# A second planner that alternates backward and forward rounds, and six banks of exponentials, in a two-layer streaming encoder step

## The chip, the cores and the metric

The kernel runs on one core of one Trainium2 chip. The metric is the device time of one execution in microseconds; lower is better. The kernel before took 3009.69 us as the median of three runs (3009.36 to 3010.79).

## The reference

The function is one inference step of a two-layer hybrid encoder for 1024 prompt tokens and 8 x 16 sample tokens (1152 rows, width 1024). All inputs and outputs are float32. Each layer does the following to `x`:

```
h = RMSNorm(x) @ w_in                      # split among three parallel groups
A: gMLP:  gelu(u) * (tril(W_s) @ RMSNorm(gelu(v)) + b_s)      4 groups x 64, chunks of 128
B: conv:  swish(LayerNorm(depthwise_conv31(a * sigmoid(gate))))              width 256
C: latent attention: 8 heads, q and k RMS-normed and rotated, keys and values from a
   128-wide latent, mask in blocks of 64 frames; the sample group also reads a past of 128
x += concat(A, B, C) @ w_out
x += softmax(qm @ mem_k) @ mem_v @ w_mo    # 4 heads x 128 into 256 memory tokens
x += relu(RMSNorm(x) @ w_ff1)^2 @ w_ff2    # hidden 4096
```

It returns `x` for both groups and the new caches (latent, rotary keys, conv state, memory keys and values, gMLP rows).

## The kernel before

A product that needs float32 accuracy is done as three TensorE matmuls: each operand is split into a high part, rounded to the type `float32r`, and a low part, and `mm3` adds high x high, high x low and low x high in one PSUM bank. Smaller products (softmax weights times values, transposes, statistics) are plain float32 matmuls. All matmuls are issued by the helper `mm` (L707) and all transposes by `tr` (L730). The other lines that the profile names are helpers, too: ScalarE activations `act` (L589) and copies (L606), VectorE two-operand instructions `vtt` (L610), `stt` (L679), reductions `red` (L683), scalar instructions `vts` (L671), splits (L750), GpSimd two-operand instructions `ptt` (L614) and memsets (L695), and DMAs on SyncE's queue (L699).

Each layer runs in stages: the mixer's input products; the attention stage, in which the gMLP, the convolution, the latent attention of four pairs of heads, the sample group's attention and the early parts of the out-projection overlap; the rest of the out-projection; memory cross-attention; and the feed-forward part, in which the up-projection uses a scheme with seven products instead of eight.

Some parts of the attention stage matter here. `attention` makes query, key and value rows per tile of 128 tokens ("tok"): matmuls, then sums of squares on ScalarE, an addition on VectorE, a power on GpSimd (`small_rstd`), scaling on ScalarE, rotation on VectorE. `heads` then transposes those tiles on TensorE. `maxima` finds the row maxima of the scores. `units` computes scores of 256 queries against 256 keys in one PSUM bank and their exponentials into a buffer of 512 words; `values` multiplies these with the values. `PTS` bounds how many such buffers of exponentials exist between `units` and `values` (L1978). `mix` is the gMLP's spatial product; its operand passes through a power on GpSimd (`pow_rstd`), too. `conv` runs 31 taps per half as VectorE instructions of 128x1024 (`stt`) for the prompt, and `taps` runs 31 for the sample group, each a ScalarE scaling and a GpSimd addition of 128x128. The result of the convolution goes to the out-projection's last part (`mixer_out`, since `REST` holds parts 2, 3, 6 and 7).

The order of all this is planned twice, while the program is built. The first planner (`plan`) runs the parts above as coroutines with priorities against a table of costs: it places every instruction at a time, and gives out the buffers of two arenas in SBUF (21000 and 36048 words per partition) and the eight PSUM banks. The list `trace` holds its instructions with their times. The second planner (`fix_order`) finds what each instruction must wait for, from the buffers and banks that it reads and writes, so that a reuse of a buffer is kept as the first planner had it. It then lets `in_order` simulate the engines again, SyncE's DMAs as an engine of their own: at each step the engine that is free first takes, of its instructions that are ready, the one with the lowest key. The result is an order for each engine, and it is fixed by dependences. The simulation has TensorE's clock (`array`), instructions that use part of the array (`narrow`), and VectorE and GpSimd that hold each other up (`holds`). The key before is

```
key = [t - URGE * r for (t, _), r in zip(self.trace, rest)]      # URGE = 0.05
```

where `t` is the first planner's time and `rest` the longest chain of costs and delays from the instruction to the end.

Of the kernel before, what the change touches and what calls it, by code (L numbers as in the profile page):

```python
# [41 lines left out]
QK = 10240  # L42
PTS = 5
FK = 3072
# [25 lines left out]
TICK = 10240.0 / 3  # L70
WARM = 3060
URGE = 0.05

# [199 lines left out]
class Enc:  # L273
# [39 lines left out]
    def array(self, t, cost, cols):  # L313


        c0 = cols / cost
        if t < self.tick * TICK:
            self.tick, self.cols_out = 0, 0.0
        while True:
            i = int(t // TICK)  # L320
            if i > self.tick:
                self.warm = i == self.tick + 1 and self.cols_out >= WARM
                self.tick, self.cols_out = i, 0.0
            f = 1.0 if self.warm else 2.0
            d = min(cost * f, (i + 1) * TICK - t)
            cost -= d / f
            self.cols_out += c0 * d / f
            if cost < 1e-6:
                return t + d
            t = (i + 1) * TICK + 1e-6  # L330
# [23 lines left out]
    def fix_order(self):  # L354


        n = len(self.trace)
# [31 lines left out]
        prev = {}  # L389
        for i in self.in_order(preds):  # L390
            ins = self.trace[i][1]
            if ins.engine in prev:
                self._after(ins, prev[ins.engine])
            prev[ins.engine] = ins
# [11 lines left out]

    def in_order(self, preds):
        n = len(self.trace)
        succ, left, ready = [[] for _ in range(n)], [len(p) for p in preds], [0.0] * n
        for i, p in enumerate(preds):  # L410
            for j in p:
                succ[j].append(i)
        engs = {r[0] for r in self.real}
        rest = [0.0] * n
        for i in reversed(range(n)):
            e = self.real[i][0]
            rest[i] += self.real[i][1]
            for j in preds[i]:
                rest[j] = max(rest[j], rest[i] + (0.0 if e == "PE" == self.real[j][0] else BEHIND[self.real[j][0]]))
        key = [t - URGE * r for (t, _), r in zip(self.trace, rest)]  # L420
        soon, now, free = {e: [] for e in engs}, {e: [] for e in engs}, {e: 0.0 for e in engs}
# [4 lines left out]
        while len(out) < n:  # L426
# [27 lines left out]
            else:  # L454
# [6 lines left out]
                free[e] = end  # L461
            out.append(i)
            for j in succ[i]:
                left[j] -= 1
                if e != "PE" or self.real[j][0] != "PE":
                    ready[j] = max(ready[j], end + BEHIND[e])
                if not left[j]:
                    heapq.heappush(soon[self.real[j][0]], (ready[j], j))
        return out

# [2388 lines left out]
```

## Time and profile before

| | us |
|---|---|
| median of three runs | 3009.69 |
| the profiled execution's own time | 3009.8 |
| its span, first to last instruction | 3008.0 |
| TensorE busy | 2920.9 (97%) |
| VectorE busy | 2118.2 (70%) |
| ScalarE busy | 1417.4 (47%) |
| GpSimd busy | 357.1 (12%) |
| mean granted TensorE clock | 0.979 |

In the profile PE is TensorE, PEld its weight loads, DVE VectorE, ACT ScalarE, POOL GpSimd and SP SyncE, whose queue issues the DMAs. A matmul's end is modelled, and TensorE's work is pipelined, so "busy" is not "at its peak". A granted clock of 1.00 is 2.4 GHz and 0.5 is 1.2 GHz. A wait is put down to the instruction that released it; "issue" means that the profile shows no releaser. The attention stages lie at about 150 to 526 us (layer 0) and 1654 to 2030 us (layer 1), the feed-forward stages at about 677 to 1504 and 2181 to 2970 us.

### The profile page before, as it was taken

The page shows a single profiled execution, that of the slowest core. Times are in us where ns is not written, and L with a number is a line of the kernel's source. Part 1 is how long each engine was busy: PE and PEld are TensorE (multiplying, and loading weights), DVE is VectorE, ACT ScalarE, POOL GpSimd, SP SyncE. Part 2 cuts the span into 40 slices and gives each one's busy share as a digit, 9 for nine tenths or more (in the row PEclk, how much of TensorE's full clock was granted, in tenths as well). Part 3 has the DMA queues.
Part 4 walks back from the last instruction along what each step waited for, and adds up shares of the span by engine and source line. Part 5 has one row for each costly group of instructions (what it writes and reads, how often), then busy time and mean ns, then how long its engine had stood idle before and what let it go on. Part 6 is the DMA issues. An engine that isn't in the chain of part 4 may idle for free.

```text
span 3008.0 us, 52427 instructions
## 1 busy us (share of the span) xinstructions
PE 2920.9 (97%) x19708; PEld 2807.8 (93%) x19708; DVE 2118.2 (70%) x4568; ACT 1417.4 (47%) x3762; POOL 357.1 (12%) x427
## 2 busy tenths in 40 slices
PE   8989999999999999999999789999999999999999
PEld 8988988979999999999999688989799999999999
DVE  8986767668655577677898867676687555777775
ACT  7566775466544452111364666664665444521110
POOL 0743220000000000000044422120100000000000
PEclk9989998999999999999999889999999999999999
DMA  6302215433232254222333010453333323532221
GB/s 208 113 30 79 66 45 166 153 120 120 101 125 95 106 185 126 90 90 76 111 99 96 26 36 28 136 182 124 123 113 125 110 91 119 181 121 90 90 73 64
DMA packets 156110, 318.14 MB, mean 106 GB/s; under 512 B 22864, under 2 KB 79824, under 8 KB 155600
## 3 DMA queue, kind: packets, MB, share of 16 engines
q1 hardware_dynamic: 155856, 314.79, 31.4%
q8 instruction: 155, 2.54, 0.3%
q14 instruction: 99, 0.81, 0.1%
HBM read 225.94 MB, written 88.80 MB: 105 GB/s over the span
## 4 chain that ended last, share of the span: by engine, by line
PE 87%; DVE 6%; ACT 4%; POOL 1%; issue 1%; DMA 0%; SPq 0%; DVEq 0%; POOLq 0%; ACTq 0%
PE bank L707 84%; PE bank L730 3%; ACT arena_f L589 3%; DVE arena_f L679 1%; POOL arena_f L614 1%; DVE arena_f L610 1%; DVE arena_r L610 1%; DVE arena_f L683 1%; DVE arena_r L679 1%; ACT arena_r L589 1%; ACT L582 0%; DVE arena_r L750 0%; ACT arena_r L606 0%; DVE arena_f L671 0%; DVE bank L691 0%
## 5 line engine op out<-in xcount | busy, mean ns | idle before, releaser
L707 PE MATMUL bank<-arena_r 128*128 128x384 f32 (+7 forms) x16464 | 2671.5, 321 | 38.8 <-DVE arena_r L750 9.3
L707 PEld LDWEIGHTS bank<-arena_r 128*128 128x128 f32 (+2 forms) x16464 | 2539.8, 190 | 103.8 <-ACT arena_f L589 21.2
L610 DVE TENSOR_TENSOR arena_f<-arena_f,bank 128x384 f32<-128x384 f32 (+1 forms) x1286 | 667.3, 529 | 409.9 <-PE bank L707 404.5
L606 ACT CAST arena_r<-arena_f 128x512 fp32r<-128x512 f32 (+5 forms) x547 | 387.8, 729 | 866.9 <-PE bank L707 799.2
L610 DVE TENSOR_TENSOR arena_r<-arena_f,arena_r 128x512 fp32r<-128x512 f32 (+7 forms) x608 | 496.3, 827 | 148.9 <-PE bank L707 124.3
L589 ACT ACTIVATE arena_f<-arena_f 128x384 f32<-128x384 f32 (+5 forms) x628 | 374.8, 620 | 230.0 <-DVE arena_f L610 171.4
L614 POOL TENSOR_TENSOR arena_f<-arena_f 128x128 f32<-128x128 f32 (+6 forms) x298 | 327.3, 1106 | 837.0 <-DVE arena_f L610 284.6
L589 ACT ACTIVATE arena_f<-bank,arena_f 128x64 f32<-128x64 f32 (+7 forms) x774 | 272.6, 424 | 202.1 <-PE bank L707 68.7
L610 DVE TENSOR_TENSOR arena_f<-arena_f 128x384 f32<-128x384 f32 (+11 forms) x832 | 299.0, 371 | 71.5 <-ACT arena_f L589 62.8
L589 ACT ACTIVATE arena_f<-bank 128x64 f32<-128x64 f32 (+6 forms) x682 | 207.7, 349 | 82.6 <-PE bank L707 44.0
L707 PE MATMUL bank<-arena_f 128*128 128x65 f32 (+7 forms) x2344 | 228.4, 290 | 11.1 <-issue 7.9
L679 DVE SCALAR_TENSOR_TENSOR arena_f<-arena_f 128x1024 f32<-128x1024 f32 (+3 forms) x236 | 221.2, 949 | 3.9 <-POOL arena_f L614 1.6
L707 PEld LDWEIGHTS bank<-arena_f 128*128 128x128 f32 (+2 forms) x2344 | 188.1, 158 | 30.7 <-issue 14.0
L730 PE MATMUL bank<-arena_f 128*128 128x128 f32 (+2 forms) x900 | 162.3, 287 | 33.4 <-ACT arena_f L589 23.8
L730 PEld LDWEIGHTS bank<-arena_f 128*128 128x128 f32 (+2 forms) x900 | 111.7, 142 | 61.4 <-ACT arena_f L589 31.4
L695 POOL MEMSET arena_f<- 128x8 f32 (+3 forms) x125 | 30.6, 251 | 973.5 <-DVE arena_r L610 760.7
L606 ACT COPY arena_f<-bank 128x288 f32<-128x288 f32 (+4 forms) x272 | 104.7, 387 | 76.0 <-PE bank L707 62.4
L683 DVE TENSOR_REDUCE arena_f<-bank 128x1 f32<-128x512 f32 (+4 forms) x224 | 119.4, 555 | 10.2 <-PE bank L707 9.5
L589 ACT ACTIVATION_READ_ACCUMULATOR arena_f<-bank 128x1 f32 x396 | 94.1, 275 | 0.0
L610 DVE TENSOR_TENSOR arena_r<-bank,arena_r 128x256 fp32r<-128x256 f32 (+3 forms) x114 | 57.8, 511 | 34.6 <-ACT arena_r L606 33.6
L679 DVE SCALAR_TENSOR_TENSOR arena_r<-bank,arena_f,arena_r 100x512 fp32r<-100x512 f32 (+3 forms) x92 | 65.9, 725 | 17.9 <-ACT arena_r L589 17.2
L589 ACT ACTIVATE arena_r<-bank,arena_f 100x512 fp32r<-100x512 f32 (+3 forms) x92 | 61.7, 690 | 28.6 <-PE bank L730 28.3
(24 smaller groups left out, 538.6 us busy)
## 6 DMA issues: line engine op xcount, KB each, us to landing
arena_f<-w SPq DMA_DIRECT2D x140, 512.0 KB, 3.6
hscr<-arena_f SPq DMA_DIRECT2D x64, 576.0 KB, 3.2
arena_f<-hscr SPq DMA_DIRECT2D x96, 384.0 KB, 3.6
xscr<-arena_f SPq DMA_DIRECT2D x96, 192.0 KB, 1.9
arena_f<-xscr SPq DMA_DIRECT2D x48, 384.0 KB, 4.1
arena_f<-xscr SPq DMA_DIRECT2D x72, 192.0 KB, 2.5
xscr<-arena_f SPq DMA_DIRECT2D x36, 384.0 KB, 2.3
arena_f<-mkc SPq DMA_DIRECT2D x32, 256.0 KB, 3.1
```

The source lines that it names most:

```text
L589: i = self.nc.scalar.activation(out, in_, func, **kw)
L606: self.nc.scalar.copy(out, in_)
L610: self.nc.vector.tensor_tensor(out=out, in0=a, in1=b, op=op)
L614: self.nc.gpsimd.tensor_tensor(out=out, in0=a, in1=b, op=op)
L679: self.nc.vector.scalar_tensor_tensor(out, a, s, b, op0=o0, op1=o1)
L683: self.nc.vector.tensor_reduce(out, in_, axis=AX.X, op=op, **kw)
L695: self.nc.gpsimd.memset(ap, val)
L707: self.nc.tensor.matmul(out, a, b, start=start, stop=stop, **kw)
L730: self.nc.tensor.transpose(out, in_, self.ident)
```

## The change

`PTS` goes from 5 to 6. In the second planner `URGE` and the sum `rest` are gone. `best_order` calls `in_order` seven times. The first time the key is the first planner's time. `in_order` now also returns when each instruction ends. `latest` then simulates the engines backward from the end: an instruction is ready when all that depend on it are placed, and of the ready ones of an engine that with the latest end in the forward round is taken; its key for the next forward round is its start in that backward schedule, counted back from the end (a negative number, the lowest for what must start first). The backward round uses the recorded costs and delays, without the clock, the narrow matmuls' columns and the engines' mutual hold. Of the seven orders the one whose last instruction ends first is kept. `array`'s state is set back at the start of each round instead of by a comparison of times.

```diff
-PTS = 5
+PTS = 6
...
-URGE = 0.05
+ROUNDS = 7
...
         c0 = cols / cost
-        if t < self.tick * TICK:
-            self.tick, self.cols_out = 0, 0.0
         while True:
...
         prev = {}
-        for i in self.in_order(preds):
+        for i in self.best_order(preds):
             ins = self.trace[i][1]
...
-    def in_order(self, preds):
+    def best_order(self, preds):
+        key = [t for t, _ in self.trace]
+        best = None
+        for _ in range(ROUNDS):
+            out, ends = self.in_order(preds, key)
+            if best is None or max(ends) < best[0]:
+                best = max(ends), out
+            key = self.latest(preds, ends)
+        return best[1]
+
+    def latest(self, preds, ends):
         n = len(self.trace)
+        left, ready = [0] * n, [0.0] * n
+        for p in preds:
+            for j in p:
+                left[j] += 1
+        engs = {r[0] for r in self.real}
+        soon, now, free = {e: [] for e in engs}, {e: [] for e in engs}, {e: 0.0 for e in engs}
+        for i in range(n):
+            if not left[i]:
+                heapq.heappush(soon[self.real[i][0]], (0.0, i))
+        start, todo = [0.0] * n, n
+        while todo:
+            t, e = min((free[e] if now[e] else max(free[e], soon[e][0][0]), e) for e in engs if now[e] or soon[e])
+            while soon[e] and soon[e][0][0] <= t:
+                i = heapq.heappop(soon[e])[1]
+                heapq.heappush(now[e], (-ends[i], i))
+            _, i = heapq.heappop(now[e])
+            _, cost, _, tile = self.real[i]
+            free[e] = t + (30.0 if tile else cost)
+            start[i] = -free[e]
+            todo -= 1
+            for j in preds[i]:
+                left[j] -= 1
+                ej = self.real[j][0]
+                ready[j] = max(ready[j], free[e] + (0.0 if e == "PE" == ej else BEHIND[ej]))
+                if not left[j]:
+                    heapq.heappush(soon[ej], (ready[j], j))
+        return start
+
+    def in_order(self, preds, key):
+        n = len(self.trace)
+        self.tick, self.cols_out, self.warm = 0, 0.0, False
+        ends = [0.0] * n
         succ, left, ready = [[] for _ in range(n)], [len(p) for p in preds], [0.0] * n
...
         engs = {r[0] for r in self.real}
-        rest = [0.0] * n
-        for i in reversed(range(n)):
-            e = self.real[i][0]
-            rest[i] += self.real[i][1]
-            for j in preds[i]:
-                rest[j] = max(rest[j], rest[i] + (0.0 if e == "PE" == self.real[j][0] else BEHIND[self.real[j][0]]))
-        key = [t - URGE * r for (t, _), r in zip(self.trace, rest)]
...
             out.append(i)
+            ends[i] = end
...
-        return out
+        return out, ends
```

## Rows read from the trace of the kernel before

**Rows 1.** Page, parts 1 and 2: TensorE's busy time; granted clock in 40 slices.
```profile
PE 2920.9 (97%) x19708; PEld 2807.8 (93%) x19708; DVE 2118.2 (70%) x4568; ACT 1417.4 (47%) x3762; POOL 357.1 (12%) x427
...
PEclk9989998999999999999999889999999999999999
```

**Rows 2.** Busy time by stretch: stretch, its length, busy us (instructions), clock, DMA share, GB/s.
```profile
150.40:526.40 376.00, 348.96 (x2742) 319.65 (x2741) 274.03 (x844) 250.90 (x1050) 107.23 (x144) 0.92 0.24 77
1654.40:2030.40 376.00, 334.15 (x2603) 305.03 (x2602) 264.40 (x835) 242.99 (x1012) 102.32 (x131) 0.92 0.24 82
676.80:1504.00 827.20, 826.59 (x5440) 823.97 (x5439) 565.90 (x1020) 311.87 (x510) 0.26 (x2) 1.00 0.33 111
2180.80:2932.80 752.00, 752.00 (x5015) 750.41 (x5014) 506.27 (x898) 279.17 (x446) 0.00 (x0) 1.00 0.33 111
```

**Rows 3.** Waits of TensorE: who waited for whom, us in total, times, longest.
```profile
PE bank L730 <- ACT arena_f L589: 23.8, 15, 11.0
PE bank L707 <- DVE arena_r L750: 9.3, 1, 9.3
...
PE bank L707 <- issue: 7.9, 1, 7.9
```

**Rows 4.** Busy time in stretches at clock 0.5: layer 0's sum; layer 1's first and sum.
```profile
sum 58.03, PE 49.08 PEld 43.39 DVE 52.78 ACT 39.49 POOL 19.69; mean PE 8.18 PEld 7.23 DVE 8.80 ACT 6.58 POOL 3.28
...
1670.03:1690.51 20.48, 14.66 (x101) 13.18 (x103) 17.16 (x44) 12.91 (x68) 10.80 (x14) 0.77 0.00 1
...
sum 61.43, PE 53.20 PEld 47.11 DVE 47.77 ACT 35.86 POOL 22.77; mean PE 7.60 PEld 6.73 DVE 6.83 ACT 5.12 POOL 3.25
```

**Rows 5.** Timeline, 1645 to 1685 us: start, length, engine, instructions, idle time before and releaser.
```profile
1659.98 11.59 DVE L679 SCALAR_TENSOR_TENSOR arena_f<-arena_f 128x1024 f32<-128x1024 f32 x9
...
1660.14 16.41 POOL L614 TENSOR_TENSOR arena_f<-arena_f 128x1 f32<-128x1 f32 x13 [0.27 <-DVE arena_f L671]
...
1663.27 0.70 PE L707 MATMUL bank<-arena_f 128*64 128x128 f32 x4 [7.90 <-issue]
1666.31 0.22 ACT L589 ACTIVATE arena_f<-bank 128x64 f32<-128x64 f32 x1 [5.69 <-POOL arena_f L614]
...
1671.48 0.42 DVE L610 TENSOR_TENSOR arena_f<-arena_f 128x6 f32<-128x6 f32 x1
...
1674.32 1.10 ACT L589 ACTIVATE arena_f<-bank,arena_f 128x64 f32<-128x64 f32 x5 [2.62 <-POOL arena_f L614]
...
1674.94 0.64 PE L730 MATMUL bank<-arena_f 128*100 128x128 f32 x2 [10.97 <-ACT arena_f L589]
```

**Rows 6.** Groups by form on VectorE, 1640 to 1680 us: busy, mean ns, idle before.
```profile
L679 DVE SCALAR_TENSOR_TENSOR arena_f<-arena_f 128x1024 f32<-128x1024 f32 x22 | 30.3, 1378 | 0.4
```

**Rows 7.** Groups by form on GpSimd, 1640 to 1680 us.
```profile
L614 POOL TENSOR_TENSOR arena_f<-arena_f 128x128 f32<-128x128 f32 x28 | 29.1, 1040 | 2.0
```

**Rows 8.** Busy time by stretch, around the crowded windows and where VectorE has time.
```profile
400.00:425.00 25.00, 25.00 (x240) 24.36 (x240) 9.93 (x37) 15.63 (x52) 5.76 (x14) 1.00 0.11 38
425.00:450.00 25.00, 19.09 (x162) 16.65 (x160) 15.05 (x65) 25.00 (x142) 10.46 (x11) 0.86 0.11 39
450.00:475.00 25.00, 18.74 (x68) 13.85 (x67) 24.43 (x68) 12.64 (x29) 3.59 (x5) 0.59 0.27 81
...
1740.00:1800.00 60.00, 54.67 (x448) 49.54 (x448) 33.38 (x115) 41.04 (x188) 17.59 (x26) 0.88 0.13 39
```

**Rows 9.** Groups by form on TensorE, whole span: products of exponentials and values.
```profile
L707 PE MATMUL bank<-arena_f 128*128 128x65 f32 x1152 | 146.5, 275 | 1.0 <-ACT arena_f L589 0.8
```

**Rows 10.** Chain of waits, 1640 to 1740 us: start, length, what.
```profile
1645.12 0.54 POOL arena_f L614
1645.73 1.34 POOL arena_f L614
...
1660.06 1.20 DVE arena_f L679
...
1667.40 1.38 DVE arena_f L679
```

## The prediction, made before the changed kernel was run

> **What bounds the kernel now.** I read the page's busy shares first, then the slices of the span, then who TensorE waited for, then busy time by stage, and last the timeline and the chain of waits around the longest stall.
>
> The page [rows 1] is to show one thing: TensorE is busy 2920.9 of 3008.0 us, and its granted clock is full almost everywhere, with dips in slices 3 to 7 of 40 (150 to 526 us) and again in slices 23 to 27 (1654 to 2030 us). Those are the attention stages of layer 0 and layer 1. The table by stage [rows 2] says it in numbers. The feed-forward stage of layer 0 has 826.59 us of TensorE in 827.20, that of layer 1 has 752.00 in 752.00, both at clock 1.00: no order of the same instructions can take anything from them. The attention stages, windows of 376.00 us each, have 348.96 and 334.15 us busy: 27.0 and 41.9 us idle, 68.9 together, out of 87.1 in the span. The remaining 18 us lie mostly at the start (the first matmul waits 9.3 us for its first weights [rows 3]) and at the end behind the last matmul.
>
> The second loss is the clock. Thirteen stretches in the two stages were granted 0.5, that is 1.2 instead of 2.4 GHz; they last 58.03 and 61.43 us, with TensorE busy for 49.08 and 53.20 of these [rows 4]. Work that is done at half clock would take half the time at the full one, so at most (49.08 + 53.20) / 2 = 51.1 us lie there. What order can reach is thus 68.9 + 51.1 = 120.0 us at the very most.
>
> The waits [rows 3] name ScalarE ahead of a transpose first: 23.8 us in 15 waits, 11.0 of it in one. The other large single one is 7.9 us with no releaser shown. Both lie in one place of layer 1 [rows 5]: between 1655.4 and 1674.9 TensorE did 0.70 us of work, 18.9 us of idle. The reader is to see the queues of the other two engines there. VectorE ran nine instructions in one go for 11.59 us, eight of them taps of the depthwise convolution (128x1024); GpSimd ran 13 instructions for 16.41 us; ScalarE stood 5.69 us and later 2.62 us behind GpSimd; and the 128x6 addition that the query/key norm needs came out of VectorE only at 1671.48, behind the taps. From 1640 to 1680 the taps are 22 instructions and 30.3 us of VectorE's 40 [rows 6], and GpSimd's 128x128 additions (the convolution of the sample group) 28 and 29.1 us [rows 7]. The result of the convolution is used only in the last part of the out-projection, at about 2030 us. So work with hundreds of microseconds of slack stood ahead of a chain that TensorE was waiting for. That is what the key of the second planner does: it is the first planner's time less 0.05 of the remaining path (line 420), and an instruction that has fallen behind its planned time has an early key, however little hangs on it.
>
> **The change part by part.** It adds and removes no arithmetic. The rounds only re-order each engine's queue, SP's with its DMAs among them, which is planned as an engine too.
>
> *The 18.9 us stall.* With the latest start in the key, taps and sample additions sink behind the short chains. What is left of the wait is the chain's own steps on GpSimd, which nothing shortens: one power for the gating norm and two for the token norms, at 16.41 / 13 = 1.26 us each [rows 5], 3.8 us. Saved: 18.9 - 3.8 = 15.1 us; bounds 0 (the buffers' reuse holds the taps where they are) and 18.9.
>
> *The half clock behind it.* The stretch 1670.03 to 1690.51 was at 0.5, with 14.66 us of TensorE in it [rows 4]. It began after the long idle time; without that I take the full clock: 14.66 / 2 = 7.3 us saved, bounds 0 and 7.3.
>
> *The taps that were pushed back* must run somewhere: 30.3 us of VectorE. From 1740 to 1800 it was busy 33.38 of 60.00 us, so 26.6 us were free, and more behind it [rows 8]. I take 0; if that cover is gone, each tap that stands before a chain costs up to its own 1.378 us [rows 6], 22 of them 30 us, which is the bound on the other side.
>
> *All other idle time and half clock of the two stages.* 68.9 - 18.9 = 50.0 us idle and 51.1 - 7.3 = 43.8 us of clock, 93.8 us. Here the profile is less kind: from 425 to 450 ScalarE is busy 25.00 of 25.00 us, and from 450 to 475 VectorE 24.43 [rows 8]. An order helps only if work moves out to 400 to 425, where VectorE did 9.93, and buffers that were placed by the first planner fix how early much of it may run. Bounds: a loss as large as a second stall of the first kind (15.1 + 7.3 = 22.4 us), and a gain of half, 46.9 us. The two stages do the same work and still differ by 14.9 us of idle time, so how the order falls is worth that much either way. I take a tenth of the 93.8, 9.4 us, near no change, because the crowded windows are the rows nearest to it.
>
> *Feed-forward stages, start and end:* 0. A changed order can cost there only where a weight comes late; VectorE is busy about two thirds of these stages and the DMA engines a third [rows 2], and that covers it. At the start the order of the first DMAs could shift the 9.3 us by about 1 us either way. If the cover of the transfers goes, one late 512 KB weight would show as a wait of the first kind, which is inside the 22.4 us above.
>
> *Six banks of exponentials.* The matmuls that use them, 1152 of 128x65, had 1.0 us of idle time in front of them in all [rows 9]: the limit of five costs 0 to 1.0 us directly. It may move other buffers (512 of 21000 words) and with them the first plan; nothing in the trace prices that, so I bound it by the 14.9 us between the two layers, either way, and take 0.
>
> *A rule that speaks against it.* Near the stall GpSimd's additions took 0.54 or 1.34 us and VectorE's taps 1.20 or 1.38 [rows 10]: each comes in a short and a long form where the other is running. The Trainium skill, "SBUF — State Buffer", section "Who interferes with whom", says that a VectorE instruction with two SBUF inputs and a GpSimd instruction that reads SBUF block each other for a whole instruction; the trace agrees with that, 0.80 us longer on GpSimd. By it, taps that move beside later powers would only carry the delay along; that is the third rival.
>
> *Sum:* 15.1 + 7.3 + 9.4 = 31.8 us less than the profiled execution's 3009.8 (span 3008.0 and 1.8 around it): 2978.0. The median of the runs is 3009.69, 0.1 below that execution, so no correction is due.
>
> **The rivals.**
> 1. *Half of the rest goes as well.* For it: the rounds attack every stall at once, and clock follows idle time. Against: the full engines at 425 to 475. 3009.8 - 22.4 - 46.9 = 2940.5.
> 2. *Nothing to measure.* The rounds keep the order that ends first by the planner's own costs. If those costs don't contain the stall at 1655 (the first round is a plain sort by planned time), the kept order can be better there and equal on the chip. For it: TensorE is 97% busy. Against: the taps in front of the chain are an order that any cost would see. 3009.
> 3. *The ports carry the delay along.* The taps and additions meet the powers of the next tokens; 28 additions at 0.80 us longer are 22.4 us of GpSimd, as much as the stall gave. Left is the tenth: 3000.4.
> 4. *Slower: chains with no reserve.* Keys by latest start place an instruction at the last moment that the planned costs allow, and each queue is in order. Where ScalarE or GpSimd takes longer than planned, the head of a queue waits and all behind it. Place: the token chains (ScalarE, VectorE, GpSimd, ScalarE, transpose) of either layer. Price: 22.4 us for each stall like the present one. For it: the 23.8 us behind ScalarE today are such heads [rows 3]. Against: the list still never leaves an engine idle when something is ready. One new stall leaves 9 us of gain; from two on it is slower: 3009.8 - 31.8 + 2 x 22.4 = 3022.8.
>
> **How the numbers follow.** The forecast, 2978.0, has 0.48; rival 1 0.10, rival 2 0.15, rival 3 0.08, rival 4 0.19. Its own range goes from 2960 (the rest gives 28 instead of 9.4) to 2996 (only the stall itself goes). The range for 8 in 10 reaches down to 2950, which leaves out most of rival 1, and up to 3017, which leaves out over half of rival 4. A measurement of this kernel tells about 0.2%, 6 us, from no change. Faster than 3003.7 are the forecast, rivals 1 and 3: 0.66; within 6 us is rival 2: 0.15; slower is rival 4: 0.19.
>
> **What would show it.** In the new profile, at the place of layer 1 where the attention's first transposes stand, the idle time ahead of TensorE should be under 5 us and no run of eight taps should stand in front of a 128x6 addition; taps should appear later, between 1700 and 1800 us. The two stages together should be some 30 us shorter, the feed-forward stages unchanged to 1 us, and the half clock of layer 1 should lose its 20 us stretch. I am wrong if the stages' idle sum stays near 69 us while the time falls (then it came from elsewhere), if a new stall over 5 us stands in either stage, or if the feed-forward stages lose their full clock.

## The result: 2927.5 us, and where 84 us came from

The changed kernel took 2927.51 us (median of four runs, 2925.45 to 2930.61) against 3010.24 for the kernel before beside it: a ratio of 0.9722, 95% interval 0.9705 to 0.9739. The forecast was 2978.0 with a range from 2950 to 3017. The sign was right. The size was not: the time is 22 us below the range.

The page of the profiled execution (2925.45 us, span 2923.7), parts 1 and 2, against [rows 1]:

```profile
PE 2883.3 (99%) x19708; PEld 2784.0 (95%) x19708; DVE 2110.4 (72%) x4584; ACT 1403.9 (48%) x3737; POOL 352.6 (12%) x427
...
PEclk9999989999999999999999999999999999999999
```

TensorE runs the same 19708 matmuls. Its busy time falls by 37.6 us (2920.9 to 2883.3) and its idle time by 46.7 us (3008.0 - 2920.9 = 87.1 to 2923.7 - 2883.3 = 40.4); together that is the 84.3 us of the span. The clock row shows where most of the 37.6 us are from: the dips in slices 23 to 27 are gone, and of those in slices 3 to 7 one is left.

Busy time by stretch, columns as in [rows 2]; the stretches are the attention and feed-forward stages at their new places:

```profile
150.40:506.60 356.20, 340.56 (x2694) 315.07 (x2693) 271.17 (x840) 242.41 (x1042) 105.13 (x143) 0.96 0.27 87
678.30:1504.00 825.70, 825.70 (x5401) 823.81 (x5400) 566.56 (x1011) 308.69 (x482) 1.92 (x5) 1.00 0.34 114
1650.20:1966.90 316.70, 309.03 (x2593) 290.92 (x2592) 250.23 (x803) 221.71 (x893) 84.53 (x113) 0.99 0.33 106
2179.00:2923.00 744.00, 740.70 (x4881) 740.30 (x4879) 473.31 (x823) 230.80 (x333) 0.00 (x0) 1.00 0.32 106
```

The attention stages went from clock 0.92 to 0.96 and 0.99, and their idle time from 27.0 and 41.9 us to 15.6 and 7.7 (length less TensorE's busy time). The stretches at half clock are seven in place of thirteen. The windows of [rows 4] do not lie on them: the clock column of its row for 1670.03 to 1690.51 says 0.77, not 0.50. The granted clock was 0.50 from 1659.08 to 1679.56, and each of the other twelve stretches, too, lies 10.95 us earlier than [rows 4] has it. The rows for the stretches as they lie, before: the one at the stall, layer 0's sum, layer 1's sum:

```profile
1659.08:1679.56 20.48, 5.04 (x23) 4.28 (x24) 18.01 (x26) 8.79 (x65) 18.63 (x17) 0.50 0.00 0
...
sum 58.03, PE 47.72 PEld 38.17 DVE 52.37 ACT 32.31 POOL 19.77; mean PE 7.95 PEld 6.36 DVE 8.73 ACT 5.39 POOL 3.29
...
sum 61.43, PE 43.83 PEld 38.33 DVE 46.65 ACT 28.47 POOL 23.87; mean PE 6.26 PEld 5.48 DVE 6.66 ACT 4.07 POOL 3.41
```

And all seven of the changed kernel as one sum:

```profile
sum 34.12, PE 31.79 PEld 27.22 DVE 29.06 ACT 22.52 POOL 9.82; mean PE 4.54 PEld 3.89 DVE 4.15 ACT 3.22 POOL 1.40
```

TensorE did 91.6 us of work at half clock before (47.72 + 43.83) and does 31.8 now; (91.6 - 31.8) / 2 = 29.9 us, most of the 37.6 us of busy time. So what got cheaper is mostly the clock, and it got better together with the idle time. The other 7.7 us are not accounted for.

Waits of TensorE, against [rows 3]:

```profile
PE bank L743 <- DVE arena_r L786: 10.2, 2, 9.8
PE bank L743 <- ACT arena_f L625: 9.2, 17, 1.5
```

The first matmul's wait is what it was (9.3 to 9.8 us). No other wait is over 2 us: the pair of 7.9 and 11.0 us in [rows 3] is gone. Line numbers are 36 higher than before: `mm` is L743, `tr` L766, `act` L625, `vtt` L646, `ptt` L650, `stt` L715.

For what follows, the steps of the span are measured between the starts of three kinds of matmul in each trace: "y", the first of 416 columns in a layer (the latent input product); the first and last of 65 columns (the values); and those of 288 columns (the up-projection). "Down" goes from the last up-projection to the start of the last matmul. All in us:

| | y to last value, layer 0 | to up | up | up to y of layer 1 | y to first value, layer 1 | to last value | to up | up | down |
|---|---|---|---|---|---|---|---|---|---|
| before | 433.7 | 218.2 | 361.9 | 476.7 | 128.6 | 329.4 | 205.7 | 360.7 | 400.9 |
| sixth bank alone | 433.7 | 221.5 | 362.4 | 476.2 | 117.6 | 299.1 | 213.9 | 360.9 | 400.1 |
| rounds alone | 409.8 | 214.3 | 361.6 | 475.8 | 125.3 | 306.6 | 205.5 | 360.7 | 400.9 |
| both (after) | 414.5 | 217.0 | 361.7 | 474.3 | 112.9 | 278.3 | 212.2 | 360.7 | 400.0 |
| taps on time | 428.2 | 217.5 | 361.7 | 474.3 | 119.7 | 287.9 | 212.3 | 360.7 | 400.0 |
| additions free | 411.9 | 214.3 | 361.6 | 475.8 | 109.8 | 316.4 | 206.5 | 360.7 | 400.9 |
| six in layer 0 only | 430.5 | 220.9 | 362.4 | 476.2 | 117.0 | 306.6 | 216.3 | 360.7 | 411.9 |

### The profile page after: what moved, and what is told of

Read it like the earlier page. It is cut to its first block, busy times and chain, and to the rows that moved or that the text cites. A ratio compares the mean times of both kernels' runs of the same rounds, so it can differ in the third digit from the quotient of the medians.

```text
span 2923.7 us, 52496 instructions
## 1 busy us (share of the span) xinstructions
PE 2883.3 (99%) x19708; PEld 2784.0 (95%) x19708; DVE 2110.4 (72%) x4584; ACT 1403.9 (48%) x3737; POOL 352.6 (12%) x427
## 4 chain that ended last, share of the span: by engine, by line
PE 93%; DVE 3%; ACT 2%; POOL 1%; issue 0%; DMA 0%; SPq 0%; POOLq 0%; DVEq 0%; ACTq 0%
PE bank L743 90%; PE bank L766 3%; ACT arena_f L625 2%; POOL arena_f L650 1%; DVE arena_f L646 1%; DVE arena_f L719 1%; DVE arena_r L646 1%; DVE arena_f L715 1%; DVE arena_r L715 0%; ACT arena_r L625 0%; DVE arena_f L707 0%; ACT arena_f L642 0%; DVE arena_r L786 0%; DMA arena_f<-x 0%; DVE bank L727 0%
## 5 line engine op out<-in xcount | busy, mean ns | idle before, releaser
L743 PE MATMUL bank<-arena_r 128*128 128x384 f32 (+7 forms) x16464 | 2654.5, 320 | 29.3 <-DVE arena_r L786 10.2
L743 PEld LDWEIGHTS bank<-arena_r 128*128 128x128 f32 (+2 forms) x16464 | 2522.2, 189 | 89.0 <-ACT arena_f L625 23.1
L646 DVE TENSOR_TENSOR arena_f<-arena_f,bank 128x384 f32<-128x384 f32 (+1 forms) x1286 | 668.5, 528 | 313.0 <-PE bank L743 310.9
L646 DVE TENSOR_TENSOR arena_r<-arena_f,arena_r 128x512 fp32r<-128x512 f32 (+5 forms) x608 | 498.4, 828 | 241.5 <-PE bank L743 216.0
L625 ACT ACTIVATE arena_f<-arena_f 128x384 f32<-128x384 f32 (+5 forms) x628 | 377.0, 621 | 231.4 <-DVE arena_f L646 171.4
L650 POOL TENSOR_TENSOR arena_f<-arena_f 128x128 f32<-128x128 f32 (+5 forms) x298 | 323.8, 1093 | 666.1 <-DVE arena_f L707 241.1
L625 ACT ACTIVATE arena_f<-bank,arena_f 128x64 f32<-128x64 f32 (+7 forms) x766 | 273.0, 419 | 148.0 <-PE bank L743 65.1
L646 DVE TENSOR_TENSOR arena_f<-arena_f 128x384 f32<-128x384 f32 (+9 forms) x832 | 296.7, 368 | 52.3 <-ACT arena_f L625 43.5
L625 ACT ACTIVATE arena_f<-bank 128x64 f32<-128x64 f32 (+5 forms) x682 | 207.6, 339 | 82.5 <-PE bank L743 58.4
L743 PE MATMUL bank<-arena_f 128*128 128x65 f32 (+7 forms) x2344 | 224.4, 286 | 3.8 <-ACT arena_f L625 3.1
L715 DVE SCALAR_TENSOR_TENSOR arena_f<-arena_f 128x1024 f32<-128x1024 f32 (+3 forms) x236 | 219.5, 942 | 1.7 <-POOL arena_f L650 0.4
L743 PEld LDWEIGHTS bank<-arena_f 128*128 128x128 f32 (+2 forms) x2344 | 185.6, 156 | 22.6 <-issue 6.8
L731 POOL MEMSET arena_f<- 128x8 f32 (+3 forms) x125 | 29.9, 244 | 1073.4 <-DVE arena_r L646 763.7
L766 PE MATMUL bank<-arena_f 128*128 128x128 f32 (+2 forms) x900 | 152.1, 276 | 3.2 <-DVE arena_f L646 1.3
L766 PEld LDWEIGHTS bank<-arena_f 128*128 128x128 f32 (+2 forms) x900 | 107.8, 137 | 23.7 <-ACT arena_f L625 6.6
L625 ACT ACTIVATION_READ_ACCUMULATOR arena_f<-bank 128x1 f32 x396 | 92.8, 262 | 0.0
L715 DVE SCALAR_TENSOR_TENSOR arena_r<-bank,arena_f,arena_r 100x512 fp32r<-100x512 f32 (+3 forms) x92 | 65.9, 722 | 17.4 <-ACT arena_r L625 16.5
L646 DVE TENSOR_TENSOR arena_r<-bank,arena_r 128x256 fp32r<-128x256 f32 (+3 forms) x114 | 57.3, 509 | 21.7 <-ACT arena_r L642 21.0
L625 ACT ACTIVATE arena_r<-bank,arena_f 100x512 fp32r<-100x512 f32 (+3 forms) x92 | 61.9, 686 | 19.2 <-PE bank L766 18.8
```

The lines of the kernel that those rows point to most:

```text
L625: i = self.nc.scalar.activation(out, in_, func, **kw)
L646: self.nc.vector.tensor_tensor(out=out, in0=a, in1=b, op=op)
L650: self.nc.gpsimd.tensor_tensor(out=out, in0=a, in1=b, op=op)
L715: self.nc.vector.scalar_tensor_tensor(out, a, s, b, op0=o0, op1=o1)
L731: self.nc.gpsimd.memset(ap, val)
L743: self.nc.tensor.matmul(out, a, b, start=start, stop=stop, **kw)
```

## The experiments

All kernels are compared with the kernel before on the same chip in the same job (its medians there were 3010.4, 3010.84 and 3011.97 us), and every ratio has its 95% interval.

### The two edits apart

`e1_rounds_only` is the changed kernel with five banks, `e2_sixth_bank_only` the kernel before with six.

```
e1:  -PTS = 6      e2:  -PTS = 5
     +PTS = 5           +PTS = 6
```

> The changed kernel with five banks of exponentials: the rounds alone. Theory R (the rounds remove the stalls, the sixth bank adds about nothing, as the 1.0 us of idle time ahead of the products with the values says): 2927 to 2935 us, and the stall at 1655 us of the kernel before is gone. Theory P (the sixth bank gives the first planner another plan, and that is a third or more of the gain): 2950 to 2975 us.

> The kernel before with six banks and the old key. Theory R: 3005 to 3015 us, the stall at 1655 us still there. Theory P: 2965 to 2985 us, since the new plan alone already shortens the attention stages.

The rounds alone: 2955.30 us, 0.9812 [0.9795, 0.9829]. The sixth bank alone: 2978.96 us, 0.9888 [0.9867, 0.9909]. From the profiled executions:

| | median | TensorE idle | TensorE busy |
|---|---|---|---|
| before | 3010.4 | 87.1 | 2920.9 |
| sixth bank alone | 2979.0 | 65.6 | 2912.4 |
| rounds alone | 2955.3 | 60.8 | 2893.2 |
| both | 2927.5 | 40.4 | 2883.3 |

31.4 and 55.1 us add up to 86.5, and both together gave 82.7 (against the kernel before beside them, 3010.24): the two edits are nearly independent in the time. The edit that I put at nothing is over a third of the gain.

The stall of [rows 5] tells more. With the rounds alone it is still there. TensorE's timeline (start, length, instructions, idle before and releaser):

```profile
1602.88 25.45 PE L743 MATMUL bank<-arena_r 128*128 128x384 f32 x185
1634.83 0.70 PE L743 MATMUL bank<-arena_f 128*64 128x128 f32 x4 [6.49 <-issue]
1645.08 0.64 PE L766 MATMUL bank<-arena_f 128*100 128x128 f32 x2 [9.56 <-ACT arena_f L625]
```

And the other engines of the same kernel at that place:

```profile
1632.41 14.27 POOL L650 TENSOR_TENSOR arena_f<-arena_f 128x1 f32<-128x1 f32 x12 [1.89 <-DVE arena_f L707]
1632.85 8.86 DVE L715 SCALAR_TENSOR_TENSOR arena_f<-arena_f 128x1024 f32<-128x1024 f32 x7
...
1636.47 0.22 ACT L625 ACTIVATE arena_f<-bank 128x64 f32<-128x64 f32 x1 [5.80 <-POOL arena_f L650]
...
1639.26 0.23 ACT L625 ACTIVATE arena_f<-bank 128x64 f32<-128x64 f32 x1 [2.27 <-POOL arena_f L650]
...
1640.31 0.24 ACT L625 ACTIVATION_READ_ACCUMULATOR arena_f<-bank 128x1 f32 x1
...
1641.63 0.41 DVE L646 TENSOR_TENSOR arena_f<-arena_f 128x6 f32<-128x6 f32 x1
```

Here is what I had misread, and [rows 5] has the same lines. The last of the six sums of squares that the 128x6 addition takes is, by the program's order, out of ScalarE at 1640.55 (1640.31 + 0.24). The addition starts at 1641.63, when the tap ahead of it is done (their rows overlap by 0.08): the taps on VectorE made it late by 1.1 us, no more. What was late is ScalarE's sums, which stood 5.80 and 2.27 us behind GpSimd. And such a sum reads a PSUM bank: nothing that GpSimd computes goes into it. Only the buffer that it writes can tie it to GpSimd. `sums`, which makes the sums of squares, takes that buffer by `tmp` from a small arena of scratch, and `taps` takes its scaled copies from the same one; the buffer comes free only when GpSimd has added the copy that was in it. No key undoes that: a reuse of a buffer is kept as the first planner had it.

With the sixth bank alone the stall is gone, by the old key. TensorE's timeline at the place:

```profile
1633.34 22.48 PE L707 MATMUL bank<-arena_r 128*128 128x384 f32 x165
1655.74 0.44 PE L707 MATMUL bank<-arena_f 128*64 128x128 f32 x4
1656.11 4.74 PE L707 MATMUL bank<-arena_r 128*128 128x384 f32 x36
```

The waits of these sums for GpSimd, in 100 us of each kernel around that place, sort the kernels by the tie (ScalarE's groups by form; a sum reads a bank alone and is 128x64 or 128x32; last, the idle time before the group and what ended it). Before, from 1600 to 1700 us:

```profile
L589 ACT ACTIVATE arena_f<-bank 128x64 f32<-128x64 f32 x24 | 5.2, 238 | 8.8 <-POOL arena_f L614 8.7
```

The rounds alone, from 1580 to 1680:

```profile
L625 ACT ACTIVATE arena_f<-bank 128x64 f32<-128x64 f32 x30 | 6.6, 239 | 9.7 <-POOL arena_f L650 9.7
```

The sixth bank alone, from 1600 to 1700:

```profile
L589 ACT ACTIVATE arena_f<-bank 128x64 f32<-128x64 f32 x32 | 7.3, 258 | 0.3 <-POOL arena_f L614 0.3
```

Both, the changed kernel, from 1600 to 1700:

```profile
L625 ACT ACTIVATE arena_f<-bank 128x64 f32<-128x64 f32 x32 | 7.5, 244 | 0.3 <-POOL arena_f L650 0.3
```

The rounds leave the wait as it was; the sixth bank takes it away. How it does so stands in the first planner's list of each kernel. The kernel before, e1, e5 and e8 have one and the same first plan; the changed kernel, e2, e3, e4, e6 and e12 share the other. With five banks the first four token tiles of layer 1 are planned 2 to 13 us behind the additions that last read their scratch. With six these tiles are planned 23 us earlier, ahead of the second half of the sample group's taps, and the last additions in their scratch are 83 to 94 us old. The reuse is still there, but only from the fifth tile on.

In layer 0 the sixth bank does nothing (433.7 us with five and with six), in layer 1 it saves 41.3 up to the last value, of which 8.2 are given back before the up-projection.

### Is the taps' key the reason for the stall?

`e5_taps_later` is the kernel before, with the instructions of the prompt's and the sample group's convolution 100 us later in the key (`who`, a new list, holds the part of the program that each comes from).

```
-key = [t - URGE * r for (t, _), r in zip(self.trace, rest)]
+key = [t - URGE * r + 100000.0 * (w in ("conv", "taps"))
+       for (t, _), r, w in zip(self.trace, rest, self.who)]
```

> The kernel before, five banks, its old key, but every instruction of the convolution (prompt and sample taps, its norm) has 100 us added to its key, so that any other ready instruction goes first. Theory K (the prediction's: taps with slack stand ahead of short chains only because the key is a planned time): the stall at 1655 us goes, 2985 to 2995 us. Theory B (the stall comes from buffers and banks that the first plan reuses, and the taps must run before them whatever the key says): no gain, 3005 to 3040 us, with idle time where the taps are then needed.

It took 3039.06 us, a ratio of 1.0098 [1.0083, 1.0113], and the stall stayed. TensorE's timeline:

```profile
1675.00 0.69 PE L708 MATMUL bank<-arena_f 128*64 128x128 f32 x4 [7.11 <-issue]
1686.66 0.64 PE L731 MATMUL bank<-arena_f 128*100 128x128 f32 x2 [10.97 <-ACT arena_f L590]
```

This settles the first term of the prediction: to sink the taps by key leaves the wait as long as it was (18.1 us for 18.9) and costs 28 us elsewhere. The tie is as it was: from 1600 to 1700 us the sums of 128x64 waited 9.9 us for GpSimd, against 8.7 before. That the additions which hold the scratch come later by their key, and so the sums that want it, is how I read this; it wasn't tested by itself.

### Does the sixth bank act through its limit, or through another first plan?

`e7_six_layer0_only` is the kernel before with a limit of six in layer 0 alone; layer 1 keeps five. The condition that ends a wait, fewer than five, is left as it was.

```
-while self.pt_out == PTS:
+while self.pt_out >= (6 if l == 0 else 5):
```

> The kernel before with the old key and a sixth bank of exponentials in layer 0 only; layer 1 keeps five. If the sixth bank itself lets layer 1's values run on: 3005 to 3012 us, layer 1 unchanged. If it only gives the first planner another plan from there on: some 2980 to 2995 us, layer 0 as before and layer 1's attention shorter, though its limit is the old one.

It took 2997.47 us, 0.996 [0.9945, 0.9975]. Layer 1, whose limit is as before, is 34.4 us shorter up to its last value (458.0 to 423.6), nearly the 41.3 of the sixth bank in both layers, and its stall is gone; another wait, of 7.10 us for VectorE, stands near its end (before 1961.02 us). Layer 0, where the limit was raised, is 3.2 us shorter. So it is not the exponentials that wait less: a changed constant early in the first planner's run gives another plan from there on, and this plan places the first token tiles of layer 1, and their scratch, as e2's does. 21.6 of the 34.4 us are given back after the last value (10.6 and 11.0 in the table), partly in one new wait for ScalarE in the last feed-forward stage, 6.00 us long.

### The tie by itself

`e8_adds_free` takes the tie out of the rounds with five banks: the additions read the window of the gated rows itself, no longer ScalarE's scaled copy in a scratch. That leaves the tap weights out of the sample group's convolution.

```
-PTS = 6
+PTS = 5
-self.ptt(o, o, pv, ALU.add)
+self.ptt(o, o, zs[:, :, k:k + 16], ALU.add)
```

> The changed kernel with five banks, and the sample group's 128x128 additions on GpSimd read the input in place of the scaled scratch buffer (this leaves the tap weights out of the sample group's convolution). The first plan is the same; what goes is the link by which ScalarE's sums for a token tile, which reuse that scratch, wait for GpSimd's additions. If that link holds the stall that the rounds alone leave in layer 1 (16 us of idle time at 1628 to 1645 and 20 us of half clock): 2928 to 2940 us. If another does (VectorE's own taps, the banks): 2950 to 2958 us and the stall is still there.

At its place the theory holds: from 1580 to 1680 us ScalarE waits for GpSimd for 1.1 us in all, none of the 4 waits over 0.4, and TensorE runs through. Its timeline:

```profile
1601.60 28.25 PE L743 MATMUL bank<-arena_r 128*128 128x384 f32 x209
1629.68 0.27 PE L766 MATMUL bank<-arena_f 128*100 128x128 f32 x1
1629.71 1.40 PE L743 MATMUL bank<-arena_r 128*128 128x256 f32 x10
1631.04 0.44 PE L743 MATMUL bank<-arena_f 128*64 128x128 f32 x4
```

From y to the first value it saves 15.5 us (125.3 to 109.8), about the stall. But the time, 2953.32 us, 0.9816 [0.9799, 0.9832], is only 2 us better than the rounds alone: between the first value and the last 9.8 us go again, in small waits and stretches at half clock. Five stretches there hold 19.9 us of TensorE's work at half clock, against 9.7 in two stretches of the rounds alone, which is about 5 of the 9.8 us; I did not find one place for the rest. By the expectation's terms this is neither case: the time is that of "another" link, but the stall is gone. The sums of the first tile start at 1616.61 us there, while the additions go on until 1633.40: what holds the sums in the rounds alone is the tie and not the additions' own length. The tie is the cause of the stall; that its removal alone would be worth the 15 us in the end is not shown.

`e9_own_scratch` is the changed kernel with a scratch of 256 words for the taps alone.

```
+own = F.alloc(256)
+self.TP = Arena(self, F.ap, own.lo, own.lo + own.n, "P")
-p = self.tmp(128)
+p = self.TP.alloc(128)
```

> The changed kernel, computing the same, with the sample taps' scaled input in a scratch of its own (256 words taken from the first arena), so that ScalarE's sums for a token tile don't share it. It makes another first plan as well; in it the limit of exponentials never binds, five or six give the same program. Theory B (in layer 1 the shared scratch ties the token tiles to GpSimd's additions, and six banks helped only by a plan without that tie): near the changed kernel without any help of a sixth bank, 2925 to 2945 us, and ScalarE waits under 6 us for GpSimd at layer 1's start. If the sixth bank itself were needed: 2950 us or more.

2950.01 us, 0.9793 [0.978, 0.9807], slower than the changed kernel by 22.5. ScalarE's waits for GpSimd are short (6.4 us in 9 waits, where under 6 was expected), and TensorE has no wait over 1.5 us from 1550 to 1700 us: the tie isn't back, nor the stall; other idle time is. The 256 words are taken from the arena, and this is another first plan again. By the expectation it came out at the bound for "the sixth bank itself" (2950 or more), though the limit never binds in this plan. So a plan without the tie can be as slow as that for other reasons, and for the size of the tie the run tells nothing.

### What the rounds do, if not at the stall

`e3_planned_time` keeps the first round alone (the key is the first planner's time), `e4_one_return` adds one backward round; `e12_longer_path` is the kernel before with six banks and twenty times the weight on the remaining path.

```
e3: -ROUNDS = 7    e4: -ROUNDS = 7    e12: -PTS = 5       -URGE = 0.05
    +ROUNDS = 1        +ROUNDS = 2         +PTS = 6       +URGE = 1.0
```

> The changed kernel with one forward round: six banks, key = the first planner's time, no return. Theory R: 3000 to 3020 us, as the kernel before, because instructions that fell behind their planned time still stand ahead of short chains. Theory P: 2965 to 2990 us.

> The changed kernel with two forward rounds and one backward round between them. If a single backward schedule carries the gain (any key that knows the engines' load from the end will do): within 15 us of the changed kernel, 2928 to 2943 us. If the repetition carries it: halfway between the one round and the seven, above 2950 us.

> The kernel before with six banks and URGE 1.0 for 0.05: the key is the planned time less the whole remaining path, with no return and no knowledge of the engines' load. If more weight on the path does what the rounds do: 2925 to 2945 us. If it takes the load of the engines, counted from the end: 2960 to 2985 us, as with six banks and the old key.

2983.25 us (0.9904 [0.9886, 0.9921]), 2926.64 us (0.972 [0.9701, 0.9738]) and 2968.78 us (0.9856 [0.9843, 0.987]). The first round is no better than the old key with six banks (2978.96). One return gives all that seven rounds give; the other five rounds give nothing on the chip. More weight on the path gives 10 of the 51.5 us that lie between the old key and the new on six banks. A key from a backward pass, in which the engines are busy with each other's work, is something other than a longer path.

`e6_taps_on_time` is the changed kernel, but the convolution's instructions keep the first planner's time as their place in each round (as time from the end).

```
-key = self.latest(preds, ends)
+key = [t - max(ends) if w in ("conv", "taps") else k
+       for k, (t, _), w in zip(self.latest(preds, ends), self.trace, self.who)]
```

> The changed kernel, but the convolution's instructions keep the first planner's time as their key in every round (counted back from the end), while all others have their latest start. Theory K: a good part of the gain goes, 2950 to 2975 us. Theory B with six banks: 2925 to 2940 us, since the convolution's place was never what cost.

2957.89 us, 0.9825 [0.981, 0.984]: 30.4 us over the changed kernel, 13.7 in layer 0 and 16.4 in layer 1. Over half of the rounds' gain (55.7 us from one round to seven) hangs on where the convolution is put. In layer 0, where y starts within 2 us of the same time in all of these kernels, the traces show how. VectorE's taps in the changed kernel from 175 to 225 us, then from 225 to 275 (count, busy, mean ns, idle before):

```profile
L715 DVE SCALAR_TENSOR_TENSOR arena_f<-arena_f 128x1024 f32<-128x1024 f32 x5 | 6.4, 1280 | 0.0
...
L715 DVE SCALAR_TENSOR_TENSOR arena_f<-arena_f 128x1024 f32<-128x1024 f32 x15 | 19.0, 1267 | 0.1
```

The kernel before has 12 and 7 there, the sixth bank alone 13 and 7, the rounds alone 4 and 16, and e6 has 10 and 7. The rounds push taps back, and e6 undoes that. In layer 1 the windows have to be counted from y, which starts 23.2 us earlier in the changed kernel. From 1616.8 to 1656.8 us, the part of the layer that 1640 to 1680 is in [rows 6] with its 22 taps:

```profile
L715 DVE SCALAR_TENSOR_TENSOR arena_f<-arena_f 128x1024 f32<-128x1024 f32 x11 | 14.8, 1345 | 0.1
```

In the 140 us ahead of that part the changed kernel has 35 taps and the kernel before 33; in the 100 us behind it 15 and 6. So here, too, taps were pushed back, but it is the other first plan that did it: the sixth bank alone has 34, 12 and 15 in the three parts, the rounds alone 32, 22 and 8, and e6 34, 13 and 14. What e6 loses in layer 1 the taps' places do not show.

The crowded windows of layer 0, columns as in [rows 8]:

```profile
400.00:425.00 25.00, 19.96 (x84) 15.34 (x84) 21.55 (x68) 14.35 (x63) 6.75 (x5) 0.75 0.23 74
425.00:450.00 25.00, 23.80 (x174) 22.12 (x173) 20.97 (x61) 15.61 (x28) 2.73 (x3) 0.86 0.45 162
450.00:475.00 25.00, 25.00 (x249) 23.90 (x248) 15.47 (x45) 15.57 (x45) 1.04 (x2) 1.00 0.45 155
```

Before, ScalarE was full in the second and VectorE in the third, while VectorE did 9.93 us in the first. Now no engine but TensorE is full in any of them, and TensorE has 68.8 us of work in the three against 62.8, at a mean clock of 0.87 against 0.82 (the mean of the three rows). Layer 0 is 19.1 us shorter up to its last value, so the windows hold later parts of it than before.

### How far other plans scatter

Two constants of the first planner that the change doesn't touch: `e10_other_window` is the changed kernel with another window for the sample group's taps, `e11_other_conv` is the changed kernel with another window for the prompt's convolution.

```
e10: -TAP_W = 6000    e11: -CONV = 14000
     +TAP_W = 8000         +CONV = 12000
```

> The changed kernel with TAP_W 8000 for 6000: the first planner may run the sample taps 8 us ahead of GpSimd in place of 6. It has nothing to do with the change; it asks how far another first plan alone moves the time under the same rounds. If the rounds repair any plan: 2925 to 2945 us. If the plan's buffers carry as much as the sixth bank did: 2950 to 3000 us.

> The changed kernel with CONV 12000 for 14000, another neutral change of the first plan, and the candidate for the lowest time. If plans differ at random around the changed kernel's: 2915 to 2945 us.

2970.92 us (0.9861 [0.9847, 0.9874]) and 2931.90 us (0.9731 [0.9718, 0.9744]). The first brings a tie back, at another instruction: not the token sums, but the sums of squares of the gMLP (128x256), whose buffers come from the same scratch. ScalarE's group, from 1600 to 1700 us:

```profile
L625 ACT ACTIVATE arena_f<-arena_f 128x256 f32<-128x256 f32 x6 | 2.5, 414 | 6.2 <-POOL arena_f L650 6.0
```

One wait of TensorE of 14.82 us for ScalarE follows there; how much of it hangs on the 6.0 us is not shown. Over the changed kernel it costs 43.4 us in all, 20.2 of them between y and the first value of layer 1, where this place is, and 28.4 in layer 0 up to the last value, of which 15.0 come back before the up-projection. The second costs 4.4. So a plan with such a tie is one that a neutral constant can give or take, and the 31.4 us of the sixth bank are of the size of that scatter (4 and 43 us, in two tries). The second was meant to beat the changed kernel and doesn't.

## Why the prediction was right in sign and wrong in size

- **The stall, 15.1 us, and the half clock behind it, 7.3: right in the place, wrong in what takes it away.** This is the step that failed first: "taps and sample additions sink behind the short chains". e1 has the new key and the stall, e2 the old key and no stall, e5 sinks the taps and keeps it. I had named the other case ("the buffers' reuse holds the taps where they are") and took it for the lower bound only. The row that decides was in [rows 5]: an ACTIVATE that reads a bank and waits 5.69 us for GpSimd. In its place the runs show a reuse of scratch that the new key leaves (waits of 16.05 us in e1 for 18.87 before) and another first plan moves. Of the signs that I had named, the stall that goes, the taps that come later and the lost 20 us stretch all came true in the changed kernel, through the sixth bank's plan: they could not tell the two edits apart, and that they came true is luck. Two sizes were misread as well. The half clock there was worth 5.04 / 2 = 2.5 us, since 14.66 us of work belong to a window 10.95 us late. And the three powers, taken at the mean of 13 mixed instructions (3.8 us), took 1.53 us for the gating norm and 1.81 on average for the two token norms, 5.2 us.
- **Six banks, 0 (bounds 14.9 either way): mis-sized.** It measured 31.4 us alone and 27.8 on top of the rounds. That the products with the values hardly wait was right, and stayed so: 2.1 us behind ScalarE in the changed kernel against 0.8 in [rows 9]. The gain came through the first plan, as I had said it might, but the bound from the two layers' difference was too small by half: e10 moves 43 us by a constant. The first planner's own list had a price for it: its last instruction is planned at 2958.1 us with five banks and at 2923.8 with six.
- **All other idle time and half clock, "a tenth", 9.4 us: mis-sized, and the largest error.** The rounds alone took 54.0 us off the span (3008.0 to 2954.0), 2.8 of it in the stall (18.87 to 16.05 us of waits): some 51 of the 93.8 us, more than the half that rival 1 had (46.9). I read the full engines at 425 to 475 us as a limit. They were the order's doing, and e6 shows over half of the gain to be the convolution's place. That 9.93 of 25 us in the window ahead of them were used was the sign to take.
- **The taps that were pushed back, 0: right in the direction; no cost was seen.** In layer 0 the rounds did it, in layer 1 the six-bank plan: there 11 taps stand where [rows 6] has 22, and 15 behind them in place of 6, 9 of these from 1700 to 1740 us.
- **Feed-forward stages, start and end, 0: right.** The up-projections moved by 0.2 and 0.0 us, the last down-projection by 0.9, the first matmul's wait by 0.5; only the way from layer 0's up-projection to y of layer 1 moved by more, 2.4 us.
- **Rival 1** came nearest, at 2940.5, but for a wrong sum: 22.4 of it were the stall, which the rounds do not remove. **Rival 2** (the kept order is no better on the chip) holds only for rounds three to seven (e4). **Rival 4** (heads of queues waiting) did not show: the longest wait for ScalarE went from 11.0 to 1.5 us.
- **Rival 3, the ports:** not so. GpSimd's additions in the changed kernel, 1640 to 1680 us, with 5 taps beside them, against 28 of 1040 ns with 22 taps in [rows 7]:

```profile
L650 POOL TENSOR_TENSOR arena_f<-arena_f 128x128 f32<-128x128 f32 x24 | 12.5, 519 | 2.5 <-ACT arena_f L625 1.2
```

That is the short form of [rows 10]; in the part of the layer that [rows 7] shows, 1616.8 to 1656.8 us here, 24 take 631 ns on average beside 11 taps. In the stall the long form helped to make the wait: of the six additions that GpSimd ran from 1661.64 to 1669.08 us, when the sums' last wait ended, five took 1.24 to 1.32 us in the trace, beside the taps, and one 0.52; at 0.52 each that wait would have ended some 3.9 us sooner (5 x 0.78), by this estimate. The Trainium skill, "SBUF — State Buffer", section "Who interferes with whom", has the two engines hold each other up; the trace agrees (0.52 us apart from the taps, up to 1.32 beside them), and the rule spoke for the change rather than against it: an order that runs taps and additions apart shortens the additions.

The half clock came out in kind as the prediction's arithmetic had it: 29.9 of the 37.6 us of busy time are work that is no longer done at half clock. But the prediction took that work from the windows that are 10.95 us late: its 51.1 us should have been 45.8 ((47.72 + 43.83) / 2), and the most that order can reach 114.7 in place of 120.0. Its own upper end, 2996, should be 2994.7 (3009.8 - 15.1).

What stays open: why the first planner, with six banks, comes to layer 1's first token tiles 23 us earlier; where the other half of e8's 9.8 us went after the first value; where the other 7.7 us of TensorE's busy time went; and why "to up" in layer 1 is 6 to 11 us longer in all kernels with the six-bank plan, with the rounds and without.

## What to carry to other kernels

Before a new order is credited with a stall, ask of the instruction that waits whether data or a buffer holds it: one that reads nothing of the engine it waits for is held by the reuse of a buffer, and two new keys on the same buffers (e1, e5) did not free it. A constant that feeds a greedy planner acts through the whole plan behind it, so look for its effect in every stage, and try a neutral constant to see how far plans scatter before you name a cause. An engine that is full in a short window, beside one in which it is half empty, is no limit yet; one backward pass that counts the engines' load gained 51.5 us on one plan where twenty times the weight on the path gained 10. And a window that is said to lie on a stretch at half clock has to show 0.50 in its own clock column; the row shown in [rows 4] says 0.77, and the work read from those windows was wrong by a tenth.

## What the runs showed of the hardware that was not expected

A GpSimd addition of 128x128 took 0.52 us apart from VectorE's taps and up to 1.32 beside them, so what the same additions hold up depends on what VectorE does beside them. And the feed-forward stage is not safe from the half clock, either: in `e7_six_layer0_only` TensorE waited 6.00 us for ScalarE before 2585.20 us, and its granted clock was 0.50 from 2585 to 2590 and 0.85 in the five us after, in a stage that has 1.00 in [rows 2] and in the changed kernel. The DMA engines were busy for 0.78 to 1.00 of the time from 2580 to 2595 us there.
